# A hybrid recurrent and attention layer: one value bank with one copy out, row halves added in DRAM, inverses by pairs, and one more gate pair as products of halves

## The chip, the cores and the metric

The kernel runs on one core of one Trainium2 chip. The metric is the device time of one execution in microseconds (us); the figure for a kernel is the median over its runs. The engines are named as the profile names them: PE (TensorE, matrix products; PEld is its weight load), DVE (VectorE), ACT (ScalarE), POOL (GpSimd) and SP (SyncE, which here only issues DMAs). L12 is line 12 of the kernel.

## What is computed

One step of a streaming layer over a prompt of 1024 rows and a sample of 64 rows, 1024 columns wide, in float32. Cut to what matters here:

```python
h = rms_norm(x, g)
z = h @ w_in            # x and gate of branch A; q, k, v, gate (GB), forget logits of branch B; merge gates MA, MB
# branch A: width-4 causal convolution, then the recurrence  h_t = a_t * h_(t-1) + x_t, times silu(gate)
# branch B, 16 heads of 64, query blocks of 128, causal:
s = einsum('qhd,khd->hqk', q, k) * HEAD_DIM ** -0.5 + cq - ck      # cq, ck: running sums of log f
y = einsum('hqk,khd->qhd', softmax(s), v) * silu(gate_b)
# each branch is projected to 1024 columns, merged by the sigmoid gates MA and MB, then one output projection,
# a norm, the residual, and a gated per-layer embedding with a norm of its own
```

## The kernel before, in words

**Precision.** A float32 product is made of three passes of a faster format: each operand is split into a high part and a low part, and PE adds high x high, low x high and high x low (`three`, L178 to L181). Splitting takes an ACT copy (the high part, L90) and a DVE subtraction (the low part, L93). Columns are tokens: 1024 of the prompt and 64 of the sample, taken in chunks of 364, 364 and 360. A *panel* is 128 output columns of a weight matrix; it is 24 steps (three chunks by eight blocks of the contraction) of three matmuls each.

**Stages.** (1) The norm, the transposition of x, and the projection of v, up to about 145 us. (2) *Quads*, to about 433 us: pairs of panels computed by seven products of half-size blocks instead of eight (`seven`, L899; the matmuls are L844, 24 to a product, 272 columns each, into tiles called quad). The list `quads` (L238 on) holds k and q, some panels for branch A, and the last `MORE` pairs of the gate panels. (3) Attention, to about 846 us: heads of 64 in blocks of 256 queries, woven with *fillers*, the remaining gate panels and a panel of branch A, as ordinary panels. (4) Branch A, the recurrence with its gates, to about 1043 us. (5) The projections of both branches and their merge, to about 1207 us, and (6) the output projection, the norms and the embedding.

**Attention.** A unit is one head and one block of 256 queries, as two halves of 128 (`par` 0 and 1). Its steps are: `scores` (s, L1203), logits on PE, the row minimum of their negative on DVE (`lowest`, tiles nm, L1184); `softmax` (L1187), exp on ACT with the row sum in sm, the inverse of sm as a power of -1 on POOL (L1193), and the scaling on POOL (L1194); `turn` (L1231), transposition on PE (tp, L1244) and the split in th (ACT) and tl (DVE); `values` (L1255), the products with v on PE (pv, L1265 and L1267). v has its high and low halves side by side, so that the upper 64 partitions of pv are to be added to the lower 64: ACT copies the upper ones out (lo), DVE adds the lower ones (y, L1293), and POOL issues the store of y to DRAM (d_y, L1297). pv is half of one PSUM bank, and two halves are used in turn.

**What sets the order.** A planner in the kernel's own code (L1033 on and L1451 on) simulates the engines. `book` puts a piece of work on an engine's timetable with costs from a table (L41 to L47), `ready` (L1380) says when a PE step's inputs are due and its room is free, and the loop at L1470 takes the first step that is ready, else a filler step. `MARGIN(ahead_by)` makes it wait longer or shorter, so that the fillers are spread evenly over attention: `ahead_by` compares the fillers used with the share of attention done. Fillers left over follow the last step. The list that results is a fixed program; each engine runs its own list in order.

**Branch A.** Per panel pair `own_gate`, `recur_in`, `convolve`, `gate` and others are called in an order written out by hand (L1716 on). For the panels here ACT makes both the high part and its negative (wl), and POOL's queue issues a DMA that adds the raw weights to wl (L297, 512 KB, an accumulating DMA from SBUF to SBUF). `spill` (L315, L1124) stores a panel's result. `branch_in` (L1819) reads d_y and the gate d_gb back in for the projection of branch B.

**The sample's rows** go the same way with one step each (`sample_scores`, `sample_turn`, `sample_values`, L1310 to L1350).

Of the kernel before, what the change touches and what calls it, by code (L numbers as in the profile page):

```python
# [8 lines left out]
F32 = mybir.dt.float32  # L9
# [5 lines left out]
P = 128  # L15
# [18 lines left out]
CW = HT // 2  # L34
PLAIN = 2

MORE = 3
W_SC = 1092
GC = 364

HOP_PE, HOP = 250.0, 90.0  # L41
D_MAX, D_LO, D_Y, D_YS = (240.0, 1.035), (130.0, 1.1), 420.0, 230.0
A_EXP, A_HI, A_LO, A_ST, A_W = (450.0, 0.85), (150.0, 0.88), 380.0, 470.0, 1060.0
G_NORM, G_INV = (260.0, 0.84), 220.0
G_DMA = 860.0
D_W = 1240.0

# [4 lines left out]


AHEAD = 4000
WAKE = 36
GA_EARLY = (1, 3, 5)
LN1P = [1.0 / 15, 1.0 / 13, 1.0 / 11, 1.0 / 9, 1.0 / 7, 1.0 / 5, 1.0 / 3]
# [16 lines left out]
def hybrid_step(tc, a, o):  # L74
# [24 lines left out]
    d_cq = dram.tile([2, NH, DEC], F32, name="d_cq")  # L99
    d_ma = dram.tile([KT, P, T], F32, name="d_ma")  # L100
    d_mb = dram.tile([KT, P, T], F32, name="d_mb")
    d_y = dram.tile([NP, P, T], F32, name="d_y")
    d_gb = dram.tile([KT, P, T], F32, name="d_gb")
    d_ga = dram.tile([KT, P, T], F32, name="d_ga")
    d_x = [dram.tile([P, T], F32, name=f"d_x{k}") for k in range(2)]
# [927 lines left out]
    def spent(ns):  # L1033
        now[0] += ns
# [21 lines left out]
    def per(cost, n):  # L1056
        return cost[0] + cost[1] * n
# [117 lines left out]
        at = book("G", smp_at[p], 490.0, lambda: pool.tensor_copy(vs[:, :, 0, :], v_smp[:, :, :]))  # L1175
        t["vs_at"] = book("G", at, 740.0, lambda: sub(pool, vs[:, :, 1, :], v_smp[:, :, :], f(vs[:, :, 0, :])))

    def tiny2(name):
        return p2.tile([P, 1], F32, name=name, tag=name, bufs=12 if name == "nm" else 8)[:, :]

    def lowest(s, w, out, m, least=-NEG):

# [1 line left out]
        return nm, book("D", now[0] + HOP_PE, per(D_MAX, w), lambda: dve.tensor_tensor_reduce(  # L1184
            out=out, in0=s[:, :w], in1=m, scale=-1.0, scalar=least, op0=ALU.add, op1=ALU.min, accum_out=nm))

    def softmax(at, nm, n, pr):  # L1187


        sm = tiny2("sm")  # L1190
        at = book("A", at, per(A_EXP, n), lambda: act.activation(  # L1191
            out=pr[:, :n], in_=pr[:, :n], func=AF.Exp, scale=-1.0, bias=nm, accum_out=sm))
        at = book("G", at, G_INV, lambda: pool.tensor_tensor(out=sm, in0=sm, in1=warm[:, :], op=ALU.pow))  # L1193
        return book("G", at, per(G_NORM, n), lambda: pool.tensor_scalar(  # L1194
            out=pr[:, :n], in0=pr[:, :n], scalar1=sm, scalar2=1.0, op0=ALU.mult, op1=ALU.mult))

    def width(q2, par):
        n = 256 * q2 + (par + 1) * P
# [4 lines left out]
    def scores(x, i, pr):  # L1203

        h, q2 = units[x]
        t = heads[h]
        half, par = divmod(i, 2)
        n, w = width(q2, par)
        q0 = (2 * q2 + par) * P
        c = slice(half * w, (half + 1) * w)  # L1210
        s = p2s.tile([P, 512], F32, name="s", tag="s")
        pe.matmul(s[:, :w], t["q1"][:, q0:q0 + P], t["k1"][:, c], start=True, stop=False)  # L1212
        pe.matmul(s[:, :w], t["q2"][:HD + 4, q0:q0 + P], t["k2"][:HD + 4, c], start=False, stop=True)  # L1213
        spent(logits_ns(w))
        nm, at = lowest(s, w, pr[:, c], mask[:, SEQ - n + c.start:SEQ - n + c.stop],
                        nm_first.pop((x, par)) if half else -NEG)
        if c.stop < n:
            nm_first[x, par] = nm
            return at, at
        return at, softmax(at, nm, n, pr)  # L1220

    turned, turned_by = {}, {}
    n_diag = [0]
# [27 lines left out]
        return book("D", at, per(D_LO, n), lambda: sub(dve, tl[:, :n], tp[:, :n], f(th[:, :n])))  # L1251

    pvs = {}
    lo_free = [0.0]
    def values(u, g, h, q2):  # L1255
        vv = heads_v[h]
        if g == 0:
            pvs[u] = pv_half()
        pv = pvs[u]
        th, tl = turned.pop((u, g))  # L1260
        high = turned_by.pop((u, g))
        def part(j, x, **kw):
            v = vv[:, 2 * g + j, :, :].rearrange("p s d -> p (s d)")
            if g < q2:
                return pe.matmul(pv[:, :256], v, x[:, j * 256:(j + 1) * 256], **kw)  # L1265
            c0 = P if j else 0
            return pe.matmul(pv[:, c0:256], v, x[:, :P] if j else x[:, P:3 * P], **kw)  # L1267

        def high_part(j, stop=False):
            tc.declare_no_dep(part(j, th, start=False, stop=stop).ins, high.ins, reason="ordered through the low part")  # L1270

        if g < q2:
            for j in range(2):
                part(j, tl, start=(g == 0 and j == 0), stop=False)
                high_part(j)
            spent(480.0)
            return
        if q2 == 0:
            part(0, tl, start=True, stop=False)
            part(1, tl, start=False, stop=False)  # L1280
            high_part(1)
        else:
            part(1, tl, start=False, stop=False)
            high_part(1)
            part(0, tl, start=False, stop=False)
        high_part(0, True)
        spent(460.0)
        lo = p2.tile([HD, 256], F32, name="lo", tag="lo", bufs=1)
        y = p2.tile([HD, 256], F32, name="y", tag="y", bufs=3)

        dst = d_y[h // 2][(h % 2) * HD:(h % 2 + 1) * HD, q2 * 256:(q2 + 1) * 256]
        at = book("A", max(now[0] + HOP_PE, lo_free[0]), A_LO, lambda: copy_act(lo[:, :], pv[HD:, :256]))
        at = book("D", at, D_Y, lambda: dve.tensor_tensor(out=y[:, :], in0=pv[:HD, :256], in1=lo[:, :], op=ALU.add))  # L1293
        v_free.popleft()
        v_free.append(at)
        lo_free[0] = at
        book("G", at, G_DMA, lambda: pool.dma_start(dst, y[:, :]))  # L1297


# [10 lines left out]
    def sample_scores(p):  # L1310
        t = smp[p]
        s = p2s.tile([P, 512], F32, name="s", tag="s")
        three(s[:, :LS], *(x[:, :] for x in qs + t["ks"]), True, False)
        pe.matmul(s[:, :LS], cs_q[:, :], cs_k[:, :], start=False, stop=True)
        spent(440.0)
        nm, at = lowest(s, LS, prs_s[:, :LS], mask_s[:, :])
        return at, softmax(at, nm, LS, prs_s)

    def sample_turn(p):
        t = smp[p]  # L1320
# [9 lines left out]
    def sample_values(p):  # L1330
        t = smp.pop(p)
        pv = pv_half()
        for i in range(2):
            pe.matmul(pv[:, :], t["vs"][:, i, 0, :], t["pt"][:, i, :, :].rearrange("p s n -> p (s n)"),
                      start=(i == 0), stop=False)
            pe.matmul(pv[:, :P], t["vs"][:, i, 1, :], t["pt"][:, i, 0, :], start=False, stop=(i == 1))
        spent(458.0)
        ys = p2.tile([P, DEC], F32, name="ys", tag="ys", bufs=1)
        ats = []
        for j in range(2):  # L1340
            js, ks = slice(j * HD, (j + 1) * HD), slice(P + j * HD, P + (j + 1) * HD)
            ats.append(book("A", now[0] + HOP_PE, per(A_HI, HD), lambda js=js, ks=ks: copy_act(ys[js, :], pv[js, ks])))
        for j, at in enumerate(ats):
            js = slice(j * HD, (j + 1) * HD)
            at = book("D", at, D_YS, lambda js=js: dve.tensor_tensor(out=ys[js, :], in0=pv[js, js], in1=ys[js, :],
                                                                     op=ALU.add))
        book("D", at, 0.0, lambda: sp.dma_start(d_y[p][:, SEQ:], ys[:, :]))
        v_free.popleft()
        v_free.append(at)

# [19 lines left out]
    due = {}  # L1372
    s_free = deque([0.0, 0.0, 0.0])
    t_free = deque([0.0, 0.0])
    v_free = deque([0.0, 0.0])
    prs = {}
    seen = {"t": 0, "v": 0}
    last_t = {u: ("t", u, q2) for u, (h, q2) in enumerate(units)}
# [62 lines left out]
            t_free.append(due[step])  # L1441
        done.add(step)

    pool.memset(warm[:, :], -1.0)
    booking = tc.manual_schedule(engines={act.engine, dve.engine, pool.engine})
    booking.__enter__()
    load_head(0)
# [16 lines left out]
    own = 0.0  # L1464
    filled = 0
    n_fill = 3 * KT * (1 + sum(e[0][0] == "r" for e in ahead) + sum(len(g[1]) for g in gates))
    head_start = n_fill
    while s_q or t_q or v_q:
        catch_up()
        times = [(i, ready(q[0])) for i, q in enumerate((s_q, t_q, v_q)) if q]  # L1470
        times = [(i, at) for i, at in times if at is not None]
        ahead_by = filled - head_start - (n_fill - head_start) * own / own_total
        best = next((i for i, at in times if at + MARGIN(ahead_by) <= now[0]), None)
        if best is None:
            at, first_ = min((at, i) for i, at in times) if times else (now[0] + 1e9, None)
            if next(fill, False):
                filled += 1
                continue
            best = first_
            now[0] = max(now[0], at)  # L1480
            catch_up()
        step = (s_q, t_q, v_q)[best].popleft()
        own += own_time(step)
        if step == ("v", 0, 0):
            head_start = filled - n_fill * own / own_total
        go(step)
    while next(fill, False):
        catch_up()
# [197 lines left out]
    class Held:  # L1686
# [8 lines left out]
        def part(self, ks, evac=None, cs=range(len(CH))):  # L1695
            for c in cs:
# [6 lines left out]
                if evac:  # L1703
                    evac(c, t0, n, self.accs[c][:, :n])

    seq = tc.manual_schedule(engines={act.engine, dve.engine})
    seq.__enter__()
    ga = own_gate(0)
# [4 lines left out]
    for k in range(0, KT - 2, 2):  # L1713
# [16 lines left out]
            run(ga)  # L1730
        own_gate(k + 1)
        xa = recur_in(k + 2)
        chunk(xa)
        chunk(xa)
        if k:
# [4 lines left out]
        mix_u(k + 1)  # L1740
        decay(k)
        xa = recur_in(k + 3)
        split_u(k + 2)
        decay_a(k)
        chunk(xa)
# [21 lines left out]
    tag, w = panel()  # L1767
    assert tag == ("f", KT - 1)
    fill = panel_steps(mm, *w, xs, lambda c, t0, n, z: spill(d_mb[KT - 1], t0, n, z))
    chunk(fill)  # L1770
    early_gate(k - 1)
    output(k - 1)
# [44 lines left out]
        return ybpool.tile([P, T], dt, name=name, tag=f"yb{i}{k}")  # L1817

    def branch_in(k, t, z):  # L1819
        sp.dma_start(t[:, :], d_y[k])  # L1820
        sp.dma_start(z[:, :], d_gb[k])
        return t, z

# [574 lines left out]
```

## Time and profile before

| | |
|---|---|
| median of 3 runs | 1431.19 us (1428.65 to 1431.42) |
| the profiled execution | 1429.49 us, of which the span is 1427.5 us |
| granted PE clock, mean | 0.998 |
| DMA queue of POOL (software) | 8160 packets, 23.25 MB, 5.9% of 16 engines' span |
| DMA queue of SP (hardware) | 119436 packets, 158.96 MB, 44.2% |

The span runs from the first to the last instruction that the profile shows; the execution's own time has some 2 us around it. Times in rows are from the span's start. A row of the timeline is start, duration, engine, line, operation; the duration of a matmul is that of its whole pipeline, so two starts tell the pace. A row of the groups has, behind the bar, the total busy time, the mean of one in ns, and the idle time ahead of these instructions with what ended it. A row of the waits has the total, the count and the longest.

### The profile page before, as it was taken

What the parts mean: (1) busy time and instruction counts of PE and PEld (TensorE: products, weight loads), DVE (VectorE), ACT (ScalarE), POOL (GpSimd) and SP (SyncE); (2) the same over time, 40 slices, a digit from 0 to 9 for tenths busy, and PEclk for the clock granted to TensorE, in tenths of its full rate; (3) what the DMA queues carried; (4) which work ended last, traced back from release to release, by engine and by line L of the source; (5) the groups of instructions that cost most, each with busy time, mean ns of one, the idle gap of its engine ahead of it and who ended that gap; (6) DMA issues with size and microseconds to landing.
All of it is one profiled execution on the core that took longest, in us unless ns stands there. A gap on an engine that the chain in (4) does not pass through costs nothing.

```text
span 1427.5 us, 25022 instructions
## 1 busy us (share of the span) xinstructions
PE 1410.8 (99%) x9217; PEld 1358.0 (95%) x9217; DVE 899.4 (63%) x1638; ACT 720.5 (50%) x1339; POOL 436.5 (31%) x652
## 2 busy tenths in 40 slices
PE   9999999999999999999999999999999999999997
PEld 8999999999999999999999999999999999888887
DVE  5564766564432666666666656898767474777654
ACT  5423544442222666666666657777544232565443
POOL 0012322233204777768776841221011000000001
PEclk9999999999999999999999999999999999999999
DMA  6667556765247764556566545564467774224211
GB/s 225 214 133 107 150 155 193 162 180 141 85 122 194 182 130 131 137 110 151 123 150 131 84 101 106 83 101 84 165 211 264 252 237 136 113 74 150 78 48 45
DMA packets 138919, 201.20 MB, mean 141 GB/s; under 512 B 24372, under 2 KB 98844, under 8 KB 137772
## 3 DMA queue, kind: packets, MB, share of 16 engines
q1 hardware_dynamic: 119436, 158.96, 44.2%
q0 software_dynamic: 8160, 23.25, 5.9%
q10 hardware_dynamic: 11200, 17.38, 3.4%
q8 instruction: 73, 1.20, 0.3%
q14 instruction: 50, 0.41, 0.1%
HBM read 131.60 MB, written 66.36 MB: 139 GB/s over the span
## 4 chain that ended last, share of the span: by engine, by line
PE 82%; DVE 6%; DMA 5%; ACT 3%; issue 3%; POOL 1%; SPq 0%; DVEq 0%; ACTq 0%; POOLq 0%
PE quad L844 17%; PE acc L179 11%; PE acc L181 11%; PE acc L180 11%; PE q L2042 5%; PE tp L1244 4%; PE pv L1265 3%; PE s L1213 2%; PE s L1212 2%; PE pv L1267 2%; PE vacc L179 1%; PE vacc L180 1%; PE vacc L181 1%; DMA w_raw<-in_w_in 1%; PE vacc L500 1%
## 5 line engine op out<-in xcount | busy, mean ns | idle before, releaser
L179 PE MATMUL acc<-xh,wh 128*128 128x364 f32 x720 | 237.6, 330 | 0.2 <-ACT st L90 0.2
L181 PE MATMUL acc<-xh,wl 128*128 128x364 f32 x720 | 235.8, 328 | 0.0
L180 PE MATMUL acc<-xl,wh 128*128 128x364 f32 x720 | 235.8, 327 | 0.0
L179 PEld LDWEIGHTS acc<-xh,wh 128*128 128x128 f32 x720 | 135.4, 188 | 1.2 <-ACT st L90 0.5
L180 PEld LDWEIGHTS acc<-xl,wh 128*128 128x128 f32 x720 | 135.3, 188 | 0.8
L181 PEld LDWEIGHTS acc<-xh,wl 128*128 128x128 f32 x720 | 135.1, 188 | 0.0
L90 ACT ACTIVATE wh<-w_raw 128x1024 fp32r<-128x1024 f32 (+1 forms) x66 | 63.4, 962 | 86.4 <-PE quad L844 34.4
L93 DVE TENSOR_TENSOR wl<-w_raw,wh 128x1024 fp32r<-128x1024 f32 (+1 forms) x55 | 62.5, 1138 | 67.6 <-ACT wh L90 47.0
L1193 POOL TENSOR_TENSOR sm<-sm,warm 128x1 f32<-128x1 f32 x136 | 79.2, 582 | 57.0 <-ACT pb L1191 21.8
L93 DVE TENSOR_TENSOR tl<-tp,th 128x512 fp32r<-128x512 f32 x96 | 65.6, 687 | 38.7 <-ACT th L90 37.9
L844 PE MATMUL quad<-xh,wh 128*128 128x272 f32 x416 | 87.4, 291 | 1.8 <-ACT p__3330 L90 1.8
L844 PE MATMUL quad<-xl,wh 128*128 128x272 f32 x416 | 86.1, 288 | 0.0
L844 PE MATMUL quad<-xh,wl 128*128 128x272 f32 x416 | 86.0, 288 | 0.0
L1191 ACT ACTIVATE pb<-pb,nm 128x896 f32<-128x896 f32 (+1 forms) x64 | 63.3, 989 | 24.0 <-DVE nm L1184 21.3
L90 ACT ACTIVATE th<-tp 128x512 fp32r<-128x512 f32 x96 | 56.4, 592 | 31.0 <-PE tp L1244 30.3
L2338 POOL TENSOR_TENSOR junk<-ple,g_ple 128x256 f32<-128x256 f32 x4 | 3.8, 956 | 213.2 <-DVE ple L2295 213.2
L1212 PE MATMUL s<-k,q 128*128 128x128 f32 (+2 forms) x192 | 67.5, 353 | 0.0
L844 PEld LDWEIGHTS quad<-xh,wh 128*128 128x128 f32 x416 | 65.3, 188 | 2.3 <-ACT p__3330 L90 2.0
L1213 PE MATMUL s<-k,q 68*128 68x128 f32 (+2 forms) x192 | 65.3, 344 | 0.5 <-issue 0.5
L844 PEld LDWEIGHTS quad<-xh,wl 128*128 128x128 f32 x416 | 65.5, 188 | 0.0
L844 PEld LDWEIGHTS quad<-xl,wh 128*128 128x128 f32 x416 | 65.4, 188 | 0.0
L1194 POOL TENSOR_SCALAR pb<-pb,sm 128x896 f32<-128x896 f32 (+1 forms) x64 | 61.5, 962 | 6.2
(744 smaller groups left out, 4230.4 us busy)
## 6 DMA issues: line engine op xcount, KB each, us to landing
w_raw<-in_w_in SPq DMA_DIRECT2D x56, 256.0 KB
q<-d_q SPq DMA_DIRECT2D x48, 256.0 KB
k<-d_k SPq DMA_DIRECT2D x48, 256.0 KB
w_raw<-in_w_in SPq DMA_DIRECT2D x64, 128.0 KB
w_raw<-in_w_branch SPq DMA_DIRECT2D x32, 256.0 KB
wl<-w_raw POOLq DMA_DIRECT2D x11, 512.0 KB, 4.5
wraw<-in_w_in SPq DMA_DIRECT2D x20, 256.0 KB
d_k<-oh ACTq DMA_DIRECT2D x16, 272.0 KB
```

Source lines behind the costliest of these rows:

```text
L90: return act.activation(out=out, in_=in_, func=AF.Copy, scale=scale)
L93: return eng.tensor_tensor(out=out, in0=in0, in1=in1, op=ALU.subtract)
L179: pe.matmul(out, ah, bh, start=start, stop=False)
L180: pe.matmul(out, ah, bl, start=False, stop=False)
L181: pe.matmul(out, al, bh, start=False, stop=stop)
L844: pe.matmul(acc[:, c, :CW], l[:, k, :], r[:, k, c * CW:(c + 1) * CW], start=(first and k == 0 and p == 0), stop=(k == 3 and p == 2), skip_ ...
L1191: at = book("A", at, per(A_EXP, n), lambda: act.activation(out=pr[:, :n], in_=pr[:, :n], func=AF.Exp, scale=-1.0, bias=nm, accum_out=sm))
L1193: at = book("G", at, G_INV, lambda: pool.tensor_tensor(out=sm, in0=sm, in1=warm[:, :], op=ALU.pow))
L1194: return book("G", at, per(G_NORM, n), lambda: pool.tensor_scalar(out=pr[:, :n], in0=pr[:, :n], scalar1=sm, scalar2=1.0, op0=ALU.mult, op1 ...
L1212: pe.matmul(s[:, :w], t["q1"][:, q0:q0 + P], t["k1"][:, c], start=True, stop=False)
L1213: pe.matmul(s[:, :w], t["q2"][:HD + 4, q0:q0 + P], t["k2"][:HD + 4, c], start=False, stop=True)
L2042: pe.matmul(acc, l[:, k, :], r[:, k, :], start=(first and k == 0 and i == 0), stop=(k == 3 and i == 2), skip_group_check=not first)
```

## The change

Four edits together:

- **One more gate pair in quads.** `MORE` goes from 3 to 4: the gate panels 0 and 1 of branch B leave the fillers and become a quad. The fillers go from 16 panels to 14 (384 steps to 336, with the 24 of the branch A panel in either number).
- **Fourteen filler steps kept back.** `TAIL = 14`: the even spreading counts 14 steps fewer.
- **One value room, one copy out.** The planner now has one room for pv (`v_free` has one entry), and y is one ACT copy of all 128 partitions by 256. The addition of the two halves leaves DVE: d_y holds both in DRAM, [head of the pair, 128, 1024], and `join_rows(k)` adds the lower to the upper with an accumulating DMA from DRAM to DRAM on POOL's queue (two heads, 64 rows, 1024 columns: 512 KB). It is called eight times in branch A. The sample's y gets a tensor of its own (d_ys), and `branch_in` loads y with three DMAs.
- **Inverses by pairs.** The exp of the first half waits, in the order of work, for that of the second; then one DVE reciprocal inverts both sums (128x2), and POOL scales both halves. The powers on POOL go.

```diff
-MORE = 3
+MORE = 4
...
-D_MAX, D_LO, D_Y, D_YS = (240.0, 1.035), (130.0, 1.1), 420.0, 230.0
-A_EXP, A_HI, A_LO, A_ST, A_W = (450.0, 0.85), (150.0, 0.88), 380.0, 470.0, 1060.0
-G_NORM, G_INV = (260.0, 0.84), 220.0
+D_MAX, INV, D_LO, D_YS = (240.0, 1.035), 165.0, (130.0, 1.1), 230.0
+A_EXP, A_HI, A_Y, A_ST, A_W = (450.0, 0.85), (150.0, 0.88), 380.0, 470.0, 1060.0
+G_NORM = (260.0, 0.84)
...
+TAIL = 14
...
-    d_y = dram.tile([NP, P, T], F32, name="d_y")
+    d_y = dram.tile([NP, 2, P, SEQ], F32, name="d_y")
+    d_ys = dram.tile([NP, P, DEC], F32, name="d_ys")
...
-    def softmax(at, nm, n, pr):
-
-
-        sm = tiny2("sm")
-        at = book("A", at, per(A_EXP, n), lambda: act.activation(
+    def powers(at, nm, n, pr, sm):
+        return book("A", at, per(A_EXP, n), lambda: act.activation(
             out=pr[:, :n], in_=pr[:, :n], func=AF.Exp, scale=-1.0, bias=nm, accum_out=sm))
-        at = book("G", at, G_INV, lambda: pool.tensor_tensor(out=sm, in0=sm, in1=warm[:, :], op=ALU.pow))
+    def inverse(at, sm, k):
+        return book("D", at, INV, lambda: dve.reciprocal(out=sm[:, :k], in_=sm[:, :k]))
+    def normal(at, n, pr, sm):
         return book("G", at, per(G_NORM, n), lambda: pool.tensor_scalar(
             out=pr[:, :n], in0=pr[:, :n], scalar1=sm, scalar2=1.0, op0=ALU.mult, op1=ALU.mult))
+    sums = {}
...
-        return at, softmax(at, nm, n, pr)
+        if par == 0:
+            sm = tiny2("sm", 2)
+            sums[x] = sm, powers(at, nm, n, pr, sm[:, :1]), pr, n
+            return at, at
+        sm, first, pr0, n0 = sums.pop(x)
+        done_ = inverse(max(first, powers(at, nm, n, pr, sm[:, 1:])), sm, 2)
+        return at, normal(normal(done_, n0, pr0, sm[:, :1]), n, pr, sm[:, 1:])
...
-        lo = p2.tile([HD, 256], F32, name="lo", tag="lo", bufs=1)
-        y = p2.tile([HD, 256], F32, name="y", tag="y", bufs=3)
-
-        dst = d_y[h // 2][(h % 2) * HD:(h % 2 + 1) * HD, q2 * 256:(q2 + 1) * 256]
-        at = book("A", max(now[0] + HOP_PE, lo_free[0]), A_LO, lambda: copy_act(lo[:, :], pv[HD:, :256]))
-        at = book("D", at, D_Y, lambda: dve.tensor_tensor(out=y[:, :], in0=pv[:HD, :256], in1=lo[:, :], op=ALU.add))
+        y = p2.tile([P, 256], F32, name="y", tag="y", bufs=3)
+        dst = d_y[h // 2, h % 2][:, q2 * 256:(q2 + 1) * 256]
+        at = book("A", now[0] + HOP_PE, A_Y, lambda: copy_act(y[:, :], pv[:, :256]))
         v_free.popleft()
         v_free.append(at)
...
-    v_free = deque([0.0, 0.0])
+    v_free = deque([0.0])
...
-    head_start = n_fill
+    shared_out = n_fill - TAIL
+    head_start = shared_out
...
-        ahead_by = filled - head_start - (n_fill - head_start) * own / own_total
+        ahead_by = filled - head_start - (shared_out - head_start) * own / own_total
...
+    def join_rows(k):
+        tc.keep_in_program_order(pool.dma_start(d_y[k][:, :HD, :], d_y[k][:, HD:, :], accum_op=ALU.add, max_dma_last_dim=4096))
...
         xa = recur_in(k + 2)
+        join_rows(k)
         chunk(xa)
...
         xa = recur_in(k + 3)
+        join_rows(k + 1)
         split_u(k + 2)
...
+    join_rows(k)
+    join_rows(k + 1)
...
-        sp.dma_start(t[:, :], d_y[k])
+        for j in range(2):
+            sp.dma_start(t[j * HD:(j + 1) * HD, :SEQ], d_y[k, j][:HD, :])
+        sp.dma_start(t[:, SEQ:], d_ys[k])
```

**DVE in attention.** The rows of DVE's program before, around the first sample step: row minima (nm, with pb and pm the rows of weights of the two halves), low halves of turned blocks (tl, diag1l), and the value add.

```order
L1184 ISA pm,nm<-s,mask 128x256
L1184 ISA nm 128x1
L1184 ISA pb,nm<-s,mask 128x512
L1184 ISA nm 128x1
L93 TENSOR_TENSOR diag1l<-tp_6234,diag1h 128x384
L1293 TENSOR_TENSOR y<-pv,lo 64x256
L1184 ISA pb,nm<-s,mask,nm 128x512
L1184 ISA nm 128x1
L93 TENSOR_TENSOR pts<-tps_6265,pts 128x2x128
```

The same place now:

```order
L1186 ISA pm,nm<-s,mask 128x256
L1186 ISA nm 128x1
L94 TENSOR_TENSOR tl<-tp_6348,th 128x512
L1186 ISA pb,nm<-s,mask 128x512
L1186 ISA nm 128x1
L1195 RECIPROCAL sm<-sm 128x2
L94 TENSOR_TENSOR diag1l<-tp_6378,diag1h 128x384
L1186 ISA pb,nm<-s,mask,nm 128x512
L1186 ISA nm 128x1
```

The add of y is gone, and a reciprocal of two sums stands between the minima of later scores and a low half of a turned block.

**POOL in branch A.** POOL's program before, from the second of the accumulating weight DMAs (wl) to the third, with small copies and memsets for the convolution (xp, st) and the final state (fin).

```order
L297 DMA wl<-w_raw 128x1024
L1569 COPY fin<-xp 128x3
L1570 COPY fin<-xp 128x3
L1545 MEMSET xp 128x3
L1546 MEMSET xp 128x1
L1548 COPY xp<-vt 128x3
L1537 MEMSET st 128x256
L297 DMA wl<-w_raw 128x1024
```

The same place now, from the second weight DMA to the fourth:

```order
L299 DMA wl<-w_raw 128x1024
L1713 DMA d_y<-d_y 2x64x1024
L1575 COPY fin<-xp 128x3
L1576 COPY fin<-xp 128x3
L299 DMA wl<-w_raw 128x1024
L1551 MEMSET xp 128x3
L1552 MEMSET xp 128x1
L1554 COPY xp<-vt 128x3
L1713 DMA d_y<-d_y 2x64x1024
L1645 COPY fin<-e 128x1
L1646 COPY fin<-e 128x1
L299 DMA wl<-w_raw 128x1024
```

A join stands right behind the second weight DMA, and another between the third and the fourth, on the same queue; the third has moved ahead of the small memsets.

More of the change, by code (lines that the diff above doesn't have):

```diff
@@ L1176, in load_sample, with tiny2 @@
         t["vs_at"] = book("G", at, 740.0, lambda: sub(pool, vs[:, :, 1, :], v_smp[:, :, :], f(vs[:, :, 0, :])))
-    def tiny2(name):
-        return p2.tile([P, 1], F32, name=name, tag=name, bufs=12 if name == "nm" else 8)[:, :]
+    def tiny2(name, n=1):
+        return p2.tile([P, n], F32, name=name, tag=name, bufs=12 if name == "nm" else 8)[:, :]
     def lowest(s, w, out, m, least=-NEG):
@@ L1253, in hybrid_step @@
     pvs = {}
-    lo_free = [0.0]
     def values(u, g, h, q2):
@@ L1287, in values @@
         spent(460.0)
-        lo = p2.tile([HD, 256], F32, name="lo", tag="lo", bufs=1)
-        y = p2.tile([HD, 256], F32, name="y", tag="y", bufs=3)
-        dst = d_y[h // 2][(h % 2) * HD:(h % 2 + 1) * HD, q2 * 256:(q2 + 1) * 256]
-        at = book("A", max(now[0] + HOP_PE, lo_free[0]), A_LO, lambda: copy_act(lo[:, :], pv[HD:, :256]))
-        at = book("D", at, D_Y, lambda: dve.tensor_tensor(out=y[:, :], in0=pv[:HD, :256], in1=lo[:, :], op=ALU.add))
+        y = p2.tile([P, 256], F32, name="y", tag="y", bufs=3)
+        dst = d_y[h // 2, h % 2][:, q2 * 256:(q2 + 1) * 256]
+        at = book("A", now[0] + HOP_PE, A_Y, lambda: copy_act(y[:, :], pv[:, :256]))
         v_free.popleft()
         v_free.append(at)
-        lo_free[0] = at
         book("G", at, G_DMA, lambda: pool.dma_start(dst, y[:, :]))
@@ L1316, in sample_scores @@
         nm, at = lowest(s, LS, prs_s[:, :LS], mask_s[:, :])
-        return at, softmax(at, nm, LS, prs_s)
+        sm = tiny2("sm", 2)[:, :1]
+        return at, normal(inverse(powers(at, nm, LS, prs_s, sm), sm, 1), LS, prs_s, sm)
     def sample_turn(p):
@@ L1337, in sample_values @@
         spent(458.0)
+        yv = p2.tile([P, 256], F32, name="y", tag="y", bufs=3)
         ys = p2.tile([P, DEC], F32, name="ys", tag="ys", bufs=1)
-        ats = []
+        at = book("A", now[0] + HOP_PE, A_Y, lambda: copy_act(yv[:, :], pv[:, :256]))
+        v_free.popleft()
+        v_free.append(at)
         for j in range(2):
             js, ks = slice(j * HD, (j + 1) * HD), slice(P + j * HD, P + (j + 1) * HD)
[L1342 to L1349, printed above, removed]
+            at = book("D", at, D_YS, lambda js=js, ks=ks: dve.tensor_tensor(
+                out=ys[js, :], in0=yv[js, js], in1=yv[js, ks], op=ALU.add))
+        book("D", at, 0.0, lambda: sp.dma_start(d_ys[p], ys[:, :]))
     units = [(h, q2) for h in range(NH) for q2 in (0, 3, 1, 2)]
@@ L1442, in go @@
         done.add(step)
-    pool.memset(warm[:, :], -1.0)
     booking = tc.manual_schedule(engines={act.engine, dve.engine, pool.engine})
@@ L1484, in hybrid_step @@
         if step == ("v", 0, 0):
-            head_start = filled - n_fill * own / own_total
+            head_start = filled - shared_out * own / own_total
         go(step)
```

## The prediction

> **What bounds the kernel now.** I began with the page's busy times.
>
> ```profile
> PE 1410.8 (99%) x9217; PEld 1358.0 (95%) x9217; DVE 899.4 (63%) x1638; ACT 720.5 (50%) x1339; POOL 436.5 (31%) x652
> ```
>
> PE is busy 99% of the span, so time can come only from fewer PE instructions or from the few places where PE waits. An average hides stages, so the busy times by stage came next. Behind each window's length stand the busy times of PE, PEld, DVE, ACT and POOL with their instruction counts. The windows are most of the two stretches of quads, then attention with the fillers woven in, then the recurrent branch.
>
> ```profile
> 145.00:264.00 119.00, 119.00 (x954) 118.45 (x954) 81.00 (x118) 52.20 (x97) 39.93 (x24) 1.00 0.58 169
> 290.00:433.00 143.00, 143.00 (x1145) 142.96 (x1144) 66.92 (x97) 40.93 (x69) 33.10 (x23) 1.00 0.45 133
> 452.00:846.00 394.00, 391.91 (x2725) 381.03 (x2724) 251.83 (x671) 254.33 (x586) 281.00 (x457) 1.00 0.59 132
> 846.00:1043.00 197.00, 196.83 (x1187) 196.53 (x1186) 160.94 (x163) 136.77 (x190) 36.22 (x77) 1.00 0.50 103
> ```
>
> PE is without a gap in all four: 2.1 us idle of 394 in attention, 0.2 us of 197 in the recurrent branch. The granted clock is 1.00. The other engines have room everywhere, least of all DVE in the recurrent branch (161 of 197). Third, the waits of PE, the engine that waits first, then who releases it, with the sum, the count and the longest.
>
> ```profile
> PE quad L844 <- ACT p__3330 L90: 1.8, 1, 1.8
> PE pv L1265 <- DVE y L1293: 1.2, 4, 0.5
> PE acc L179 <- ACT st L90: 0.2, 1, 0.2
> ```
>
> The second row is the one that the new value bank aims at, and it is small. All of PE's waits in attention and behind it together are a few microseconds: the change cannot win much by taking waits away, but it can lose much by adding one.
>
> **The change, part by part.**
>
> *One more gate pair as products of halves.* Two panels of 24 steps leave the fillers: 48 steps of three matmuls. The timeline of PE at the end of attention shows successive first matmuls of such steps.
>
> ```profile
> 844.81 0.33 PE L179 MATMUL acc<-xh,wh 128*128 128x360 f32 x1
> 845.31 0.33 PE L179 MATMUL acc<-xh,wh 128*128 128x360 f32 x1
> 845.81 0.33 PE L179 MATMUL acc<-xh,wh 128*128 128x360 f32 x1
> ```
>
> The starts are 0.50 us apart (the 0.33 us in the rows is the pipelined length, not the pace). 48 x 0.50 = 24.0 us leave attention. What comes in their place is one more quad: seven products of 24 matmuls, 168 in all. The chain of work that ended last has a long unbroken stretch of these.
>
> ```profile
> 322.08 111.44 PE quad L844 x888
> ```
>
> That is 111.44 / 888 = 0.1255 us each, so 168 x 0.1255 = 21.1 us. The balance is -2.9 us, on the path, since PE is full in both stages. The weights' extra sums go to POOL and the result's combinations to DVE; in the quads' windows POOL is busy 40 of 119 and 33 of 143 us and DVE 81 and 67, so they are hidden there. I allow 1 us for a start of the new quad like the 1.8 us wait above, as an upper bound, and take 0.
>
> *The value bank.* One bank was shared by two halves in turn; PE waits for DVE's read of the other half. Now there is one room, so the planner knows of the read, and one ACT copy empties it. The groups of the two old instructions, of the wait, and of an ACT copy as large as the new one (128x256):
>
> ```profile
> L90 ACT ACTIVATE lo<-pv 64x256 f32<-64x256 f32 x64 | 24.4, 382 | 20.4 <-PE pv L1265 9.4 <-PE pv L1267 7.9 <-PE pv L1336 1.2
> L1293 DVE TENSOR_TENSOR y<-pv,lo 64x256 f32<-64x256 f32 x64 | 26.4, 412 | 32.9 <-ACT lo L90 11.9 <-PE pv L1265 7.8 <-ACT st L90 3.9
> L90 ACT ACTIVATE st<-tpk 128x256 f32<-128x256 f32 x19 | 6.9, 379 | 5.7 <-DMA out_k_prompt<-st 5.7
> ```
>
> ACT spends 0.38 us either way, so it neither gains nor loses; DVE loses 26.4 us of adds, and the room comes free 0.41 us sooner, plus whatever DVE was late. The wait rows for L1265 total 1.2 us; what PE's weight loads waited for y comes to more.
>
> ```profile
>   PEld pv L1265: 2.1, 4
>   PEld pv L1267: 1.4, 4
> ```
>
> So the gain lies between 0 (one room instead of two halves may make the same wait at another place) and 3.5 us. I take 2.0, in the middle. At the end of attention the chain that feeds the recurrent branch is shorter by DVE's add, 0.41 us, but PE waits in that branch for only 0.2 us: nothing there.
>
> *Inverses by pairs.* POOL's powers go, and DVE does half as many reciprocals on two columns.
>
> ```profile
> L1193 POOL TENSOR_TENSOR sm<-sm,warm 128x1 f32<-128x1 f32 x136 | 79.2, 582 | 57.0 <-ACT pb L1191 21.8
> L155 DVE RECIPROCAL r_y<-r_y 128x1 f32<-128x1 f32 x16 | 2.6, 162 | 7.6 <-ACT r_y L154 7.6
> L1191 ACT ACTIVATE pb<-pb,nm 128x896 f32<-128x896 f32 (+1 forms) x64 | 63.3, 989 | 24.0 <-DVE nm L1184 21.3
> ```
>
> 72 x 0.162 = 11.7 us come onto DVE and 79.2 leave POOL (281 of 394 becomes about 202). DVE's balance in attention is 11.7 - 26.4 = -14.7. The price is order: the reciprocal stands in DVE's queue and waits for an exp of about 1 us on ACT; behind it are queued the row minima of later scores and the low halves of turned blocks, and PE waits for those low halves. The first half's weights also wait for the second half's exp. With 48 fewer fillers to put between (of 384, 12%), I charge +0.5 us; from 0 to 8 us are possible (the second rival).
>
> *Fourteen steps kept back* only shift where fillers stand; the step count is the same. Taken at 0, within 0.5 either way.
>
> *Row halves added in DRAM.* Eight accumulating DMAs of 512 KB enter POOL's queue in the recurrent branch, each right behind or between the accumulates that finish a weight panel's low half. POOL itself has 161 of 197 us free, and an issue takes it 0.87 us. The cost hangs on the DMA rings. The timeline of POOL shows the issues of three old ones.
>
> ```profile
> 868.79 0.87 POOL L297 DMA_DIRECT2D wl<-w_raw  x1 [2.85 <-ACT wl L90]
> 883.82 0.85 POOL L297 DMA_DIRECT2D wl<-w_raw  x1 [3.62 <-ACT wl L90]
> 896.72 0.90 POOL L297 DMA_DIRECT2D wl<-w_raw  x1
> ```
>
> The chain shows the first one's transit, and the answer for their line how steady the landing of all eleven is (minimum, median, maximum).
>
> ```profile
> 868.79 4.57 DMA wl<-w_raw
> ```
> ```profile
> DMA to landing us min/median/max: 4.5/4.5/4.7
> ```
>
> A join moves as many bytes as such an accumulate, so if it spreads as these do, it is off the rings 4.6 us after issue. Issued behind the first (at about 870), it has landed by 875, nine microseconds before the next accumulate is issued at 883.8; the second, issued some 2 us behind that one, lands by 891 with 5 us to spare before 896.7. So 0 for all eight. The loads of the y rows, now three where one was, wait on SP's queue for the joins, but stand late:
>
> ```profile
> L1820 SPq DMA_DIRECT2D yb_in<-d_y x6: 319/330/1166, 1049.3 to 1090.8; - x6
> ```
>
> The last two joins are issued about 1000, so these loads wait for nothing, and two more issues of 0.33 us each cost SP nothing that PE sees. Had a join taken longer, this is what it would run into:
>
> ```profile
> 891.57 0.33 PE L179 MATMUL acc<-xh,wh 128*128 128x364 f32 x1
> 891.73 0.33 PE L180 MATMUL acc<-xl,wh 128*128 128x364 f32 x1
> 891.90 0.33 PE L181 MATMUL acc<-xh,wl 128*128 128x364 f32 x1
> ...
> 903.47 0.33 PE L179 MATMUL acc<-xh,wh 128*128 128x364 f32 x1
> 903.64 0.33 PE L180 MATMUL acc<-xl,wh 128*128 128x364 f32 x1
> 903.80 0.33 PE L181 MATMUL acc<-xh,wl 128*128 128x364 f32 x1
> ```
>
> These are the first uses of the panels whose low halves were issued at 883.8 and 896.7, and land at 888.3 and 901.3: the slack is 3.6 and 2.5 us. [...] The join's outermost dimension is 2. [...] No trace of before has a POOL DMA whose outermost dimension is that small, so no run here shows it yet.
>
> **The sum.** -2.9 (pair) -2.0 (bank) +0.5 (order of inverses) +0 (steps kept back) +0 (joins) = -4.4 us against the profiled execution's 1429.5 us: 1425.1. The median of the runs lies 1.7 us above that execution, so the median to expect is **1426.8**.
>
> **The rivals.** *The joins are confined to two engines.* Place: the low halves of weight panels in the recurrent branch. Price: a 64 KB store of a y block lands after 2.3 us in the median, the 512 KB accumulate after 4.5, on rows
>
> ```profile
> DMA to landing us min/median/max: 1.9/2.3/11.7
> ```
>
> so 28 KB more on each of 16 engines takes 2.2 us, 0.079 us per KB, and a join's 256 KB on each of two engines takes 20 us; with the minimum of 1.9 it is 24; I take 22. The first join starts behind the accumulate that lands at 873.4 and ends at 895.4; the next accumulate's 32 KB on those engines need another 2.5 and land at 897.9, 6 us after PE asks at 891.9. The second join, if it falls on other engines, starts at 888.3 and ends at 910.3, and its successor lands at 912.8 where PE, by then 6 late, asks at 909.8: 3 more. On the same engines it would be 12.6 more. That is 9 to 18.6 us for two joins and 27 to 56 for the six that have an accumulate behind them (the last two have none), a time of 1454 to 1483. It decides from the point where a join holds its engines for longer than 891.9 - 2.5 - 873.4 = 16 us; spread over four engines (11 us) it would not be seen. For it speaks that the join is the only DMA of this shape; against it that every accumulate in the trace lands within 4.5 to 4.7 us, whatever else is in flight. [...] Chance 0.34.
>
> *Attention runs short of cover.* A reciprocal held behind ACT's exp delays the low halves, and PE asks for them in order. If in one of four of the 64 blocks of values PE waits as long as the longest such wait in the row on y, 0.5 us, that is 16 x 0.5 = 8 us in place of the 0.5 charged. Against it: DVE is busy only 252 of 394 us there and gets 15 lighter, and PE's idle time of 2.1 us shows that the planner hides such chains. Time 1426.8 + 7.5 = 1434.3, chance 0.10.
>
> *The pair's saving is all there is*, the bank's waits only move: -2.9 + 0.5 = -2.4, a median of 1428.8. This belongs to the forecast's own spread.
>
> **How the numbers follow.** Forecast, joins hidden: 0.56, its own range 1422 to 1430. About 0.2% (2.9 us) is what a measurement of this kernel can tell from no change, so faster means below 1428.3 and slower above 1434.1. Of the forecast's 0.56, 0.44 lie below 1428.3 and 0.12 within. The second rival's 0.10 fall half within and half above; the first rival's 0.34 lie above. Faster 0.44, same 0.17, slower 0.39. The range has to take in the cheaper half of the first rival: 1421 to 1470, which leaves out its dearer half, 0.17, and a sliver below.
>
> **What would show each step.** In the profile after: the matmuls of L844 up by 168 and the filler matmuls down by 144; the wait of PE on y gone and none in its place on y's ACT copy or on tl in attention, with PE's idle time there below 2 us; the landing of the joins near 4.6 us; PE's idle time in the recurrent branch still under 0.5 us. The forecast is wrong if a join lands after more than 16 us and PE waits on wl there, or if PE's idle time in attention grows by more than 4 us.

## The result, and the profile after

The changed kernel takes 1489.32 us (4 runs, 1488.39 to 1490.33) against 1430.66 for the kernel before (4 runs), a ratio of 1.041 with a 95% interval of 1.039 to 1.043: 59 us slower. The profiled execution took 1489.42 us with a span of 1487.7. The forecast was 1426.8 and the range ended at 1470.

The stages tell where it went. These are the windows of the changed kernel in attention and from the recurrent branch on (length; busy times of PE, PEld, DVE, ACT, POOL; granted PE clock; DMA share; GB/s):

```profile
475.00:846.00 371.00, 370.51 (x2609) 362.45 (x2608) 238.52 (x680) 243.08 (x573) 199.65 (x322) 1.00 0.60 147
846.00:1100.00 254.00, 202.80 (x1141) 199.47 (x1140) 150.94 (x155) 130.73 (x183) 40.98 (x79) 0.89 0.50 96
```

and the last one in the kernel before:

```profile
846.00:1100.00 254.00, 253.62 (x1527) 252.96 (x1526) 195.60 (x205) 159.79 (x212) 47.27 (x98) 1.00 0.58 145
```

Attention is as full as forecast. In the second window PE is idle for 51.2 us where it was idle for 0.4, and its clock is 0.89 where it was 1.00. PE's waits in the changed kernel:

```profile
PE acc L183 <- DMA wl<-w_raw: 30.8, 4, 11.6
PE gacc L181 <- ACT uh L91: 16.5, 2, 10.8
PE held L181 <- DVE sg_e L1677: 2.1, 1, 2.1
PE quad L846 <- ACT p__3331 L91: 2.0, 1, 2.0
```

The first row is the wait that the first rival named: the low half of a weight panel, finished by the accumulating DMA. The second is one that the prediction did not name. The landing times of the joins (line 1713) and, from the page, of the weight accumulates behind them:

```profile
L1713 POOL DMA_DIRECT2D d_y<-d_y x8: 1425/1777/2869, 866.9 to 1046.8; - x8
...
DMA to landing us min/median/max: 25.8/27.6/29.1
```
```profile
wl<-w_raw POOLq DMA_DIRECT2D x11, 512.0 KB, 5.5
```

A join lands after 25.8 us at the least; an accumulate of the same 512 KB landed after 4.5 in the kernel before. The accumulates' median of 5.5 hides the late ones: the one issued at 881.20 (below) is landed when PE goes on at 895.46. The timeline of PE shows the first of the waits. The last matmul waits for the low half, and what follows starts 0.30 us apart, not 0.166:

```profile
887.72 0.33 PE L181 MATMUL acc<-xh,wh 128*128 128x364 f32 x1
887.89 0.33 PE L182 MATMUL acc<-xl,wh 128*128 128x364 f32 x1
895.46 0.67 PE L183 MATMUL acc<-xh,wl 128*128 128x364 f32 x1 [7.24 <-DMA wl<-w_raw]
895.93 0.50 PE L181 MATMUL acc<-xh,wh 128*128 128x364 f32 x1
896.23 0.51 PE L182 MATMUL acc<-xl,wh 128*128 128x364 f32 x1
```

The join had been issued at 866.85 and the accumulate at 881.20, as POOL's timeline has it:

```profile
865.11 0.88 POOL L299 DMA_DIRECT2D wl<-w_raw  x1 [2.86 <-ACT wl L91]
866.85 1.43 POOL L1713 DMA_DIRECT2D d_y<-d_y  x1 [0.86 <-issue]
...
881.20 0.93 POOL L299 DMA_DIRECT2D wl<-w_raw  x1 [10.41 <-ACT xp L91]
```

The second wait, on uh, leads through ACT. ACT's timeline before it:

```profile
929.20 1.21 ACT L1617 ACTIVATE r<-r,sp 128x1092 f32<-128x1092 f32 x1
945.22 1.06 ACT L91 ACTIVATE wh<-w_raw 128x1024 fp32r<-128x1024 f32 x1 [14.81 <-DMA w_raw<-in_w_in]
946.31 1.06 ACT L91 ACTIVATE wl<-wh 128x1024 fp32r<-128x1024 f32 x1
947.27 1.10 ACT L91 ACTIVATE uh<-u 128x1092 fp32r<-128x1092 f32 x1
```

ACT stands for 14.8 us in front of a weight panel that has not arrived, and uh, which does not need that panel, is queued behind. That raw panel came on SP's hardware ring, not on POOL's. In the chain such loads are the long pieces; the same load in the chain of before took 5.52 us.

```profile
871.27 24.32 DMA w_raw<-in_w_in
...
985.61 23.80 DMA w_raw<-in_w_in
```
```profile
874.86 5.52 DMA w_raw<-in_w_in
```

So two kinds of transfer were late: what is queued behind a join on its own ring, and loads on another ring.

### The profile page after: what moved, and what is told of

The parts are those of the page before. It is cut to its first block, busy times and chain, and to the rows that moved or that the text cites. A ratio compares the mean times of both kernels' runs of the same rounds, so it can differ in the third digit from the quotient of the medians.

```text
span 1487.7 us, 24997 instructions
## 1 busy us (share of the span) xinstructions
PE 1420.7 (95%) x9241; PEld 1368.7 (92%) x9241; DVE 891.8 (60%) x1655; ACT 713.1 (48%) x1331; POOL 366.0 (25%) x521
## 4 chain that ended last, share of the span: by engine, by line
PE 78%; DMA 13%; DVE 3%; issue 3%; ACT 2%; SPq 1%; POOL 0%; ACTq 0%; DVEq 0%; POOLq 0%
PE quad L846 19%; PE acc L181 10%; PE acc L183 10%; PE acc L182 10%; DMA w_raw<-in_w_in 7%; PE q L2057 5%; PE tp L1256 4%; PE pv L1276 3%; PE s L1219 2%; PE s L1218 2%; PE pv L1278 2%; DMA wl<-w_raw 2%; PE vacc L181 1%; PE vacc L182 1%; PE vacc L183 1%
## 5 line engine op out<-in xcount | busy, mean ns | idle before, releaser
L183 PE MATMUL acc<-xh,wl 128*128 128x364 f32 (+1 forms) x672 | 224.1, 333 | 30.8 <-DMA wl<-w_raw 30.8
L181 PE MATMUL acc<-xh,wh 128*128 128x364 f32 (+1 forms) x672 | 228.2, 340 | 1.0 <-ACT st L91 1.0
L182 PE MATMUL acc<-xl,wh 128*128 128x364 f32 (+1 forms) x672 | 223.1, 332 | 0.0
L181 PEld LDWEIGHTS acc<-xh,wh 128*128 128x128 f32 x672 | 129.2, 192 | 2.3 <-ACT st L91 1.3
L182 PEld LDWEIGHTS acc<-xl,wh 128*128 128x128 f32 x672 | 129.1, 192 | 1.0
L846 PE MATMUL quad<-xh,wh 128*128 128x272 f32 x448 | 94.6, 293 | 2.0 <-ACT p__3331 L91 2.0
L846 PE MATMUL quad<-xl,wh 128*128 128x272 f32 x448 | 93.4, 290 | 0.0
L846 PE MATMUL quad<-xh,wl 128*128 128x272 f32 x448 | 93.1, 289 | 0.0
L1256 PE MATMUL tp<-ident,pb 128*128 128x128 f32 x416 | 63.1, 272 | 0.0
L182 PE MATMUL acc<-ybl,wh 128*128 128x364 f32 (+1 forms) x192 | 62.9, 328 | 0.0
```

Of the source, the lines that this page charges most:

```text
L181: pe.matmul(out, ah, bh, start=start, stop=False)
L182: pe.matmul(out, ah, bl, start=False, stop=False)
L183: pe.matmul(out, al, bh, start=False, stop=stop)
L846: pe.matmul(acc[:, c, :CW], l[:, k, :], r[:, k, c * CW:(c + 1) * CW], start=(first and k == 0 and p == 0), stop=(k == 3 and p == 2), skip_ ...
L1256: pe.transpose(tp[:, i * P:(i + 1) * P], pr[par][:, kb * P:(kb + 1) * P], ident[:, :])
```

## The experiments

The theory after the result (A): a join with two as its outermost dimension sits on two DMA engines and holds them for some 25 us, and whatever needs these engines waits. Rivals: (B) the accumulation in DRAM is slow by itself; (C) POOL's work of issuing is what costs. All changes below are made to the changed kernel, or to the one named. A ratio behind a time is to the kernel before, run beside it each time, with medians from 1429.8 to 1430.1 us.

**Rows outermost.** The same joins with the row as the outer dimension:

```diff
-pool.dma_start(d_y[k][:, :HD, :], d_y[k][:, HD:, :], accum_op=ALU.add, max_dma_last_dim=4096)
+pool.dma_start(d_y[k][:, :HD, :].rearrange("h p n -> p h n"), d_y[k][:, HD:, :].rearrange("h p n -> p h n"),
+               accum_op=ALU.add, max_dma_last_dim=4096)
```

> Same joins, same bytes, but the rows are the outer dimension (64 x 2 x 1024 in place of 2 x 64 x 1024). Theory A (a join sits on two engines and holds them for some 25 us, and what is queued there waits): the joins land in about 5 us, PE waits on wl for under 1 us in the recurrent branch, and the time falls to the forecast without that cost, 1424 to 1429. Theory B (the accumulation from DRAM to DRAM is slow in itself, whatever the shape): joins still land after 20 us or more and the time stays above 1470. Theory C (what costs is POOL's work of issuing joins, 1.4 to 2.9 us each): unchanged but for a few us, above 1480.

Measured: 1426.81 us, 0.9978 of before (0.9970 to 0.9987). The joins of this kernel:

```profile
L1713 POOL DMA_DIRECT2D d_y<-d_y x8: 928/1323/1353, 863.5 to 991.9; - x8
...
DMA to landing us min/median/max: 6.5/8.0/8.6
```

The bytes are the same; the landing falls from 27.6 to 8.0 us and the time by 62.5 us. B falls. So does C: the median issue on POOL takes 1.3 us in place of 1.8, which is some 4 us over the eight joins. (The order of POOL's program also shifts a little: the third weight accumulate goes back behind the small memsets. In the two runs below with the low halves on DVE no weight accumulate is left to shift, and the shape still makes most of the difference.) The forecast of 5 us for the landing was too low. Most of these joins are issued about half a microsecond behind a weight accumulate of the same size (the first at 863.53, behind one at 862.96), and both are in flight together: POOL's queue then keeps 95.6% of 16 engines busy (shown below). With no accumulates on that queue, in the run with the low halves on DVE and the rows outermost, the joins landed after 5.6 us in the median.

**No joins.**

```diff
-        tc.keep_in_program_order(pool.dma_start(d_y[k][:, :HD, :], ...))
+        pass
```

> No joins at all: the addition of the lower row halves is left out, so branch B takes in the upper halves alone; everything else as in the changed kernel. This is the floor that a hidden join can reach. Theory A: within 1 us of the kernel with the rows outermost, 1424 to 1429. If it is more than 3 us below that kernel, joins cost something even when they are spread. If it stays above 1470, the joins are not the cause at all.

Measured: 1423.55 us, 0.9957 (0.9944 to 0.9971). The floor is 3.3 us below the kernel with the rows outermost, just over the 3 us set down: spread joins still cost something where they stand.

**Each join in two pieces.**

```diff
+        for i in range(0, HD, 32):
+            lo, hi = d_y[k][:, i:i + 32, :], d_y[k][:, HD + i:HD + i + 32, :]
+            tc.keep_in_program_order(pool.dma_start(lo, hi, accum_op=ALU.add, max_dma_last_dim=4096))
```

> Each join as two DMAs of 2 x 32 x 1024: the outer dimension stays 2, but each has half of the rows. Theory A with successive DMAs on different pairs of engines: each holds its pair for about 11 to 13 us, below the 16 us at which PE begins to wait by the prediction's sum, so at most a few us are lost: 1425 to 1440. Theory A with both on the same pair: as the changed kernel, about 1489. Theories B and C: about 1489 too, or more, with twice the DMAs.

Measured: 1459.29 us, 1.021 (1.020 to 1.022): outside both of theory A's figures. The pieces, and PE's waits:

```profile
DMA to landing us min/median/max: 15.4/16.6/18.4
```
```profile
PE gacc L181 <- ACT uh L91: 8.8, 2, 4.6
PE acc L183 <- DMA wl<-w_raw: 6.9, 4, 2.9
PE held L181 <- ACT wh L91: 3.0, 1, 3.0
```

Two pieces issued within 0.8 us of each other land together, not one after the other, and the wait for low halves falls from 30.8 to 6.9 us. How many engines carry a join can be read from the view of the DMA queues. These rows are POOL's queue (q0: packets, MB, share of 16 engines) while the changed kernel has one join in flight (872 to 880 us), this kernel two pieces (870 to 876), and the kernel with the rows outermost one join and the accumulate ahead of it (864 to 870):

```profile
q0 software_dynamic: 48, 0.20, 12.3%
q0 software_dynamic: 67, 0.27, 23.7%
q0 software_dynamic: 259, 0.99, 95.6%
```

12.3% of 16 engines is two engines that hardly pause, 23.7% is four, and 95.6% is nearly all. So a join as changed sits on two engines, its two pieces sit on two pairs, and with the rows outermost it is spread. But the wait through ACT behind a raw panel stays (8.8 us on uh, of 16.5; raw loads of 13.03 and 13.17 us in the chain): the threshold of 16 us had been worked out for the wrong transfer.

**Low halves on DVE, with the joins as changed.**

```diff
-            if ahead[0][0][0] in "xgf":
+            if False:
```

> Joins stay on 2 x 64 x 1024, but the low halves of weight panels in the recurrent branch are made by a subtraction on DVE (11 x 1.1 us) in place of the ACT copy and the accumulating DMA, so nothing of POOL's ring is waited for by PE there. Theory A1 (only the DMAs behind a join in the same ring wait): the waits go, 1425 to 1440 with what DVE costs. Theory A2 (all rings of the two engines wait, the raw weight loads on SP's ring too): raw loads still land 20 us late where a join is in flight, and the time stays at 1450 to 1485.

> The control to the run with the low halves on DVE: the same subtraction on DVE, but with the rows outermost in the joins. Theory A2 (the raw loads suffered from the two engines): the raw loads are on time and the time is 1424 to 1432, some 45 us below that run's 1473.7. If it stays above 1460, the subtractions on DVE were what cost there, and the loads were not.

Measured: 1473.70 us (1.031, 1.029 to 1.032) with the joins on two engines, and 1428.12 (0.9988, 0.9979 to 0.9996) with the rows outermost and the same subtractions. With no weight accumulate left that could queue behind a join, 45.6 us of the 62.5 remain. PE's waits, and a raw load of the chain, in the first of the two:

```profile
PE gacc L181 <- ACT uh L91: 29.6, 2, 15.5
PE held L181 <- ACT wh L91: 4.8, 1, 4.8
```
```profile
915.49 22.01 DMA w_raw<-in_w_in
```

A2 holds: a raw load on SP's ring takes 22 us beside a join on two engines, though it is queued behind nothing of POOL's. The trace of the changed kernel shows a join and the rest of a raw load side by side: from 878 to 880 us the queues of POOL (q0) and SP (q1) move 12 packets each and take 13.7% of 16 engines between them, about two engines:

```profile
q0 software_dynamic: 12, 0.05, 12.3%
q1 hardware_dynamic: 12, 0.01, 1.4%
```

By these shares a packet of the join (4096 bytes) holds its engine for 0.33 us and one of the load (512 bytes) for about 0.04. A raw panel of 512 KB is 1024 such packets, 64 for each of 16 engines if they are spread evenly. An estimate from these shares for the two engines of the join, with as many packets of the one as of the other as in those 2 us, is 64 x 0.37 = 23.7 us; the load in the chain above took 24.32.

**The last two joins earlier.** In the kernel with the rows outermost, PE waits once more than in the one without joins, at the start of the branch projections:

```profile
1041.12 0.33 PE L182 MATMUL held<-yal,wh 128*128 128x364 f32 x1
1041.29 0.32 PE L183 MATMUL held<-yah,wl 128*128 128x364 f32 x1
1043.44 0.43 PE L181 MATMUL held<-yah,wh 128*128 128x360 f32 x1 [1.83 <-DVE st_a L1879]
```

```diff
+        if k:
+            join_rows(KT - 2 + (k == 4))     # behind join_rows(k) in the panel loop
...
-    join_rows(k)
-    join_rows(k + 1)
```

> As the kernel with the rows outermost, but the last two joins, which there stand together just ahead of the loads for the branch projections, are made in the second and the third round of the panel loop. Theory D (the 3.2 us between that kernel and the one without joins come from these two joins holding up the loads behind them, so that a gate comes late and PE waits 1.8 us at 1041 us and then runs at half its pace for some 4 us): 1423 to 1425. Rival E (each spread join costs some tenths of a us wherever it stands, by sharing the engines): 1426 to 1428.

Measured: 1424.15 us, 0.9960 (0.9947 to 0.9972), within 0.6 us of no joins at all, and the wait is down to 0.2 us, as theory D has it. It is 0.4% below the kernel before.

**The other three edits, one at a time.** First the bank:

```diff
+        at = book("A", max(now[0] + HOP_PE, lo_free[0]), A_Y, lambda: copy_act(lo[:, :], pv[HD:, :256]))
+        at = book("D", at, 420.0, lambda: dve.tensor_tensor(out=y, in0=pv[:HD, :256], in1=lo[:, :], op=ALU.add))
-    v_free = deque([0.0])
+    v_free = deque([0.0, 0.0])
```

> The value bank as before (two halves of a bank in turn, ACT copies the upper partitions, DVE adds), so that no join is needed and none is made; the other three edits stay. Compare with the kernel without joins (1423.6). The prediction gave the bank 2.0 us (0 to 3.5): 1424 to 1427. If the waits of PE on y come back in the trace and the time does not move, the bank is worth nothing.

Measured: 1435.01 us, 1.0032 (1.0022 to 1.0041), 11.5 us above the kernel without joins, far more than the 2.0 set down. PE's waits in attention:

```profile
PE pv L1277 <- DVE y L1304: 2.0, 4, 0.6
PE pv L1277 <- ACT lo L91: 1.4, 3, 0.5
PE s L1219 <- DMA q<-d_rows: 1.2, 1, 1.2
```

and the same windows of attention without and with the old bank:

```profile
475.00:842.00 367.00, 366.56 (x2584) 358.54 (x2584) 236.00 (x678) 240.41 (x570) 198.10 (x320) 1.00 0.61 147
```
```profile
475.00:842.00 367.00, 362.38 (x2526) 349.99 (x2525) 253.65 (x733) 242.64 (x561) 200.62 (x313) 1.00 0.59 134
```

PE idles 4.6 us in place of 0.4, and it issues 58 matmuls fewer in the same window. By the pages the profiled spans are 8.9 us apart: PE is idle for 5.1 us more and busy for 3.8 us more (1409.5 against 1405.7 for the same 9241 matmuls), and where the second part comes from stays open. A likely reason for the waits, not shown by a run of its own, is that the old bank and the new reciprocals together put two waits on ACT into DVE's queue. That combination did not exist in the kernel before, where the waits on y came to 3.5 us at most.

Then the inverses as powers on POOL, with the rows outermost and with the last joins earlier:

```diff
-        return book("D", at, INV, lambda: dve.reciprocal(out=sm[:, :k], in_=sm[:, :k]))
+        return book("G", at, 220.0, lambda: pool.tensor_tensor(out=sm[:, :k], in0=sm[:, :k], in1=warm[:, :], op=ALU.pow))
```

> As the kernel with the rows outermost, but the inverses are again powers on POOL, one for each half, right after its exp. The prediction charged the new order +0.5 us, with 0 to 8 possible. If pairing costs cover, this one is faster than 1426.8 by up to a few us; if POOL's 79 us of powers were in the way, it is slower. Expected: within 1 us of it, 1426 to 1428.

> As the kernel with the last two joins earlier, but with the inverses as powers on POOL, one for each half. With the two gains added (0.8 and 2.7 us) 1423.3; if pairing makes no difference, 1424.2, within 0.7.

Measured: 1425.98 (0.9968, 0.9956 to 0.9981) and 1423.90 (0.9958, 0.9946 to 0.9970), 0.8 and 0.3 us below their pair-wise counterparts, inside the intervals: with the new bank, no gain and no loss by pairing shows.

The gate pair back in the fillers (`MORE = 3`), likewise twice:

> As the kernel with the rows outermost, but MORE = 3: the gate pair goes back from the quads to the fillers. By the prediction's sum the pair is worth 2.9 us (24.0 of fillers against 21.1 of products), so 1429 to 1430.5, 2 to 4 us above the kernel with the rows outermost (1426.8). Rival: the pair as a quad pays for a start of its own or for lost cover in attention, then the two are within 1 us of each other.

> As the kernel with the last two joins earlier, but MORE = 3: the pair's worth once more, without the wait at 1041 us. By the prediction's sum 2.9 us slower: 1427. If the pair's gain is eaten by the waits at the start of attention (1.6 and 0.5 us in the kernel with the rows outermost, 0.9 without the pair), 1424.5 to 1425.5.

Measured: 1427.71 (0.9980, 0.9971 to 0.9989) and 1424.80 (0.9967, 0.9955 to 0.9979), 0.9 and 0.7 us above. The intervals of about 1.3 us to either side leave the pair's worth open between nothing and the 2.9 forecast; both times it was the low end. In the second of these kernels PE has no idle time in attention; with the pair as a quad it has 1.4:

```profile
470.00:842.00 372.00, 372.00 (x2615) 364.75 (x2615) 229.40 (x645) 234.84 (x553) 191.32 (x307) 1.00 0.63 144
```
```profile
470.00:842.00 372.00, 370.57 (x2607) 362.20 (x2606) 236.02 (x678) 242.18 (x573) 198.53 (x320) 1.00 0.61 148
```

So about half of the 2.9 is given back as idle time; 1.3 us of it is one wait at the start of attention.

No steps kept back (`TAIL = 0`):

> As the kernel with the last two joins earlier (1424.2), but TAIL = 0, so the fillers are spread over all of attention. The prediction took this part at 0 within 0.5: 1423.5 to 1425. Rival: the kept-back steps fill a wait at the end of attention, then this one is 1 to 3 us slower and PE shows a wait there.

Measured: 1425.60 (0.9975, 0.9965 to 0.9985), 1.4 us above and just outside the 1423.5 to 1425 set down. The intervals overlap, so a gain by keeping steps back is not shown; the trace has a new wait of 0.7 us on tl at the end of attention, which is what the rival looked for.

## Why the prediction was wrong, step by step

**The joins: the step that failed.** "If it spreads as these do, it is off the rings 4.6 us after issue ... So 0 for all eight." It does not spread. With the rows outermost the same joins land after 8.0 us and the time is 1426.8; as the change has them, 27.6 us and 1489.3. The two engines of the first rival stood on no trace of the kernel before; the runs show them: a third of the landing time when only the shape changes, two pieces that land together after 16.6 us, and a join that keeps 12.3% of 16 engines busy, which is two. The chance of 0.34 for this rival was too low: the one argument against it, that all eleven accumulates land alike (4.5 to 4.7 us), came from DMAs of another shape and said nothing on this one.

**The rival's price: too small, for two reasons.** It put 27 to 56 us on a first wait of 6 us and on wl alone. The first wait is 7.24 us, and the waits on wl come to 30.8 us, near the lower end. But the sum looked only at what is queued in the same ring. (1) The raw loads on SP's ring, beside a join on two engines, took 22 to 24 us for 5.5; the prediction has no term for this sharing. ACT waits for them in order, and PE's 16.5 us on uh are behind that. The run with the low halves on DVE shows that this alone is worth 45.6 us, so the two overlap. (2) With each of the five long waits comes a stretch at half pace (granted clock 0.50), which no sum had: 68 matmuls between 840 and 1110 us start 0.30 us apart and not 0.166, some 9 us. By the pages, PE is idle for 67.0 us of the span here and for 18.2 with the rows outermost, and busy for 1420.7 and 1408.2 with the same 9241 matmuls. The 48.8 us of idle time and the 12.5 of slower work make up the 61.3 between the two profiled spans.

**The threshold of 16 us** was roughly right for wl (6.9 us of waits left at 16.6 us of landing) and missed the raw loads.

**The pair**, -2.9: 0.7 to 0.9 measured, with wide intervals; the count of instructions was right (PE has 9241 matmuls and had 9217, which is 168 - 144 more), and about half of the gain was given back as idle time.

**The bank**, -2.0 within 0 to 3.5: undoing it costs 11.5 us beside the other three edits. The sign was right, the size wrong: it was priced from the waits of before, and what the bank is worth depends on the other edits. That the reciprocals in the queue of the engine that would have emptied the bank are the reason is likely and not shown, and the bank alone on the kernel before was not run.

**The inverses** (+0.5) and **the steps kept back** (0): not to be told from nothing, as forecast, and the second rival did not come (PE is idle for 0.5 of 371 us in attention).

**The forecast of 1426.8** is what the kernel takes once the joins spread, 1426.81, but by luck, since errors cancel: the bank gave more, the pair less, and spread joins cost 3.3 us, of which 2.7 were the place of the last two.

## What to carry to other kernels

Look at the outermost dimension of every DMA that is added, not only at its bytes: 512 KB landed after 8 us as 64 x 2 x 1024 and after 28 as 2 x 64 x 1024. Here a transfer that held two engines delayed the loads on another queue (24.32 us for 5.52) as well as those behind it (PE waited 30.8 us for them), so its price is read from the loads with the least slack on any queue, and from what stands behind them in an in-order engine. The rows of DMAs of another shape gave no price for the join: a rival that names a shape which no row has deserves the larger chance, and one line to try both shapes.

## What the runs showed of the hardware

In the changed kernel the granted clock of PE fell to 0.50 five times between 840 and 1110 us, 2.9 to 4.7 us after the start of a wait of 5.7 to 11.6 us. The rows around the first of these waits (PE is idle from 888.2 to 895.46) are the 3.41 us in which the wait begins, the stretch at half clock, and the 6 us behind it:

```profile
887.75:891.16 3.41, 0.47 (x3) 0.17 (x1) 3.34 (x3) 1.34 (x4) 0.00 (x0) 1.00 0.26 52
891.16:901.40 10.24, 5.94 (x20) 5.94 (x21) 7.08 (x9) 5.75 (x10) 2.63 (x5) 0.50 0.59 114
901.40:907.40 6.00, 6.00 (x38) 6.00 (x38) 4.92 (x5) 3.25 (x5) 0.00 (x0) 1.00 0.25 49
```

The clock falls during the wait, at 891.16, and stays at 0.50 for 5.9 us of work behind it. Its 20 matmuls would have taken 3.2 us at the 0.158 us of the 38 behind them, so 2.8 us are lost on top of the wait. The other four stretches at 0.50 between 840 and 1110 us last 10.24, 13.65, 6.83 and 13.65 us: all are whole multiples of 3.41.

In the kernel with the rows outermost a wait of 1.83 us (1041.61 to 1043.44) was followed by a stretch of 3.41 us at half clock, and a wait of 1.82 us in the kernel before (287.7 to 289.5) by none. The rows are two successive steps of 3.41 us of each kernel, first of the one with the rows outermost, then of the one before, where they are counted back from the change of its clock at 1422.34:

```profile
1040.42:1043.83 3.41, 1.58 (x10) 1.28 (x9) 3.41 (x6) 2.00 (x3) 0.14 (x1) 1.00 0.00 0
1043.83:1047.24 3.41, 3.41 (x14) 3.41 (x13) 0.88 (x2) 0.00 (x0) 2.10 (x4) 0.50 0.87 276
```
```profile
285.70:289.11 3.41, 1.97 (x16) 1.75 (x14) 3.41 (x5) 0.95 (x2) 3.41 (x3) 1.00 0.84 172
289.11:292.53 3.42, 3.04 (x24) 3.04 (x25) 2.97 (x10) 0.54 (x2) 1.90 (x1) 1.00 0.73 263
```

The first wait lies within one step, which leaves PE idle for 1.83 us of it; the second is split over two, 1.44 and 0.38 us. With the traces of the kernel before and of the changed kernel cut into such steps from 20 us on, each of the eight steps at full clock in which PE was idle for 2.02 us or more is followed by 0.50, and none of the others, in which it was idle for 1.79 us or less, is. No run was made to vary the length of a wait.
